# Turning FFN activations and the later x in 32x32 squares on VectorE, with DMAs inside SBUF, instead of on TensorE

## The chip, the cores and the metric

The kernel runs on one core of one Trainium2 chip. The metric is device time in microseconds (us): the median of three runs. One further execution was profiled, and every row shown here is read from that execution. Engines: PE is TensorE (PEld its weight loads), DVE is VectorE, ACT is ScalarE, POOL is GpSimd, SP is SyncE, which here only issues DMAs.

## What is computed

Two layers of an encoder trunk, 256 tokens wide and 2048 channels deep, in float32. Each layer adds to x a mixer, a cross-attention into 256 memory tokens and a SwiGLU FFN with 5632 hidden channels:

```python
for i in range(DEPTH):                       # DEPTH = 2
    h = rms_norm(x, norm_mix_g[i])
    x = x + (retention_na_mixer(h, ...) if i % 2 == 0 else diff_attention_mixer(h, ...))
    m = rms_norm(mem, norm_mem_g[i])
    x = x + memory_cross_attention(rms_norm(x, norm_xattn_g[i]), m, ...)
    x = x + swiglu_ffn(rms_norm(x, norm_ffn_g[i]), w_ffn_in[i], w_ffn_out[i])

def swiglu_ffn(h, w_in, w_out):
    g, u = jnp.split(h @ w_in, 2, axis=-1)
    return (jax.nn.silu(g) * u) @ w_out
```

## The kernel before

Nearly all the time is one long list of matrix products with weights streamed from HBM, walked by `gemm`. Products are made from three matmuls in fp32r on operands split into a high and a low part (`hi*wh + hi*wl + lo*wh`). A **unit** is two 128-row slices of a weight block, for both halves of the 256 tokens: 2 x 2 x 3 = 12 matmuls of 128x512. A 1 MB weight tile `raw` serves two units. For each unit `prepare` has SP load `raw` (every second unit), ACT copy it to `wh` and DVE subtract `wl`. It runs up to three units ahead of the PE. `raw`, `wh` and `wl` have three buffers each. So the copy of one unit waits for the matmuls of the unit three before it, and the load of a `raw` waits for the subtraction of the unit five before the first of its own two.

The stationary operand of a matmul is the activation, channels on partitions, while results and x have tokens on partitions. So activations have to be turned. `turn` does that with four PE transposes (matmuls against an identity) into one PSUM tile `pt` for a half of a 512-column block, and both halves make 8 transposes for a block. Then ACT and DVE split the tile into its two parts: `gained` (with a gain per channel) for x, `split` for FFN activations.

Such work beside the main stream is held in generators run by `side`: `side.pump` after each unit lets one ready step be written, `yield n` puts the rest off by n units, and `side.drain` writes what a later unit needs. The framework's scheduler then moves instructions within each engine's list by its own reckoning, so that the order in the built program is not that of the code. Each engine, SP included, runs its list strictly in order.

The places that the change touches, each with four blocks of 512 channels of x or with one block of activations:

- **memory feed**: after `w_out`, x is turned into `hTx`, used by the product with `w_xq`. The eight units with `w_xkv` (columns 0 to 511) stand between, on the turned memory `mT`. Once in each layer. Here the units of `w_xkv` are called K1 to K8.
- **FFN feed**: during and after `w_xo` (8 units, two for each block) x is turned into `hTf`, used by `w_ffn_in`. Once in each layer. The first units of `w_ffn_in` are F1, F2, F3.
- **next-layer feed**: during the last `w_ffn_out` of layer 0, x is turned into `hT` of layer 1. Once. That product has 24 units: G1 to G24. Block 0 is complete after G10, block 1 after G12, block 2 after G18, block 3 after G24.
- **activations**: 11 blocks in each layer, one for every 16 units of `w_ffn_in`, turned by `act_T` into `aT`, used by `w_ffn_out`.

`x_block(b)` is block b of x in SBUF for both token halves, and `add_x` adds a finished product to it on DVE.

Of the kernel before, what the change touches and what calls it, by code (L numbers as in the profile page):

```python
# [10 lines left out]
F32 = mybir.dt.float32  # L11
# [5 lines left out]
P = 128  # L17
D = 2048
T = 256
# [4 lines left out]
SCALE = HD ** -0.5  # L24
LAM_INIT = 0.8 - 0.6 * math.exp(-0.3 * 1)
NEG = -1e30
FFN_GROUPS = ((0, 4), (4, 8), (8, 11))

OPENING = {2: (2, 3), 4: (-1,), 6: (4, 5), 8: (-2,), 10: (6, 7), 12: (-3,), 14: (-4,)}
# [51 lines left out]
def trunk_kernel(  # L81
# [8 lines left out]
    nc = tc.nc  # L90
# [9 lines left out]
    qk = pool("qk", 1)  # L100
    vp = pool("vp", 2)
# [3 lines left out]
    m8 = pool("m8", 1)  # L105
# [35 lines left out]
    for q in range(2):  # L141
        lo_v, hi_v = wmask[64 * q:64 * q + 64, 0:48], wmask[64 * q:64 * q + 64, 16:64]
        nc.gpsimd.affine_select(lo_v, lo_v, pattern=[[1, 48]], compare_op=ALU.is_ge,
                                fill=NEG, base=8, channel_multiplier=-1)
        nc.gpsimd.affine_select(hi_v, hi_v, pattern=[[-1, 48]], compare_op=ALU.is_ge,
# [8 lines left out]
    def gain(i, layer, k):  # L154
        c = i * 32 + layer * 16 + k
        return gcol[:, c:c + 1]
# [58 lines left out]
    side = Side()  # L215
# [24 lines left out]
    for layer in range(2):  # L240
        j = layer // 2
# [84 lines left out]
    def square_sum(dst, src):  # L326
        junk = sqp.tile([P, NB], F32, tag="sq", name="junk")
        nc.scalar.activation(junk, src, AF.Square, accum_out=dst)

    def turn(srcs, u):  # L330
        pt = ps_t.tile([P, 2, T], F32, tag="pt", name="pt")
        for j in range(2):
            for t in range(2):
                c = (2 * u + j) * P
                nc.tensor.transpose(pt[:, j, t * P:(t + 1) * P], srcs[t][:, c:c + P], ident)  # L335
        return pt

    def gained(dst, kt, src, g):
        hi, lo = dst[0][:, kt], dst[1][:, kt]
        nc.scalar.activation(hi, src, AF.Copy, scale=g)  # L340
        nc.vector.scalar_tensor_tensor(out=lo, in0=src, scalar=g, in1=hi.bitcast(F32),
                                       op0=ALU.mult, op1=ALU.subtract)
# [20 lines left out]
    def finished(tasks):  # L363
        tasks = list(tasks)
        return lambda: all(t["done"] for t in tasks)

    def feed(dst, b, u, srcs, gi, layer, ssr, then=None):
        pt = turn(srcs, u)
        for j in range(2):
            k = 4 * b + 2 * u + j  # L370
            gained(dst, k, pt[:, j], gain(gi, layer, k))
        square_sum(ssr[0][:, u, b:b + 1], srcs[u])
        if then:
            then()
        return
        yield

    def feed_x(dst, b, gi, layer, ssr, wait=0):

        then = (lambda: finish_rstd(ssr)) if b == 3 else None  # L380
        t0 = side.add(feed(dst, b, 0, x_block(b), gi, layer, ssr), wait)
        return [t0, side.add(feed(dst, b, 1, x_block(b), gi, layer, ssr, then), wait + 1, finished([t0]))]

    def split(hi, lo, src):
        nc.scalar.copy(hi, src)
        nc.vector.tensor_sub(lo, src, hi)
# [299 lines left out]
    def finish_rstd(ssr):  # L686
        ss, rstd, r2 = ssr
        nc.vector.tensor_reduce(r2, ss, axis=AX.X, op=ALU.add)
        rsqrt_mean(rstd, r2, D)
        nc.vector.tensor_mul(r2, rstd, rstd)  # L690

    def x_block(b):
        return [x_sb[:, t, b * NB:(b + 1) * NB] for t in range(2)]
# [7 lines left out]
    hT = pair(which[0], "hT")  # L701
    ssr = new_ss("ssx")
    tasks = [side.add(feed_first(hT, u), 2 * u - 2, lambda u=u: u in xts) for u in range(8)]
# [11 lines left out]
    for layer in range(2):  # L715
        j = layer // 2
        A, B = which
        oT = pair(B, "oT")
        if layer % 2 == 0:
            gate = retention_na(j, hT, ssr[1:], oT, gate)  # L720
            kts = (8, 12, 0, 4)
        else:
            nc.vector.scalar_tensor_tensor(out=tabs, in0=tdiff, scalar=-1.0, in1=tdiff, op0=ALU.mult, op1=ALU.max)
            gate = diff_attention(j, hT, ssr[1:], oT, gate)
            kts = KT4

        mT = pair(A, "mT")
        m_v = mem[0].rearrange("(t p) d -> p t d", p=P)

        def mem_block(b):  # L730
            if layer == 0:
                mb = [att.tile([P, NB], F32, tag="att", name="mb") for _ in range(2)]
                for t in range(2):
                    nc.sync.dma_start(mb[t], m_v[:, t, b * NB:(b + 1) * NB])
            mts = [att.tile([P, 2, T], F32, tag="att", name="mt") for _ in range(2)]
            for u in range(2):
                nc.sync.dma_start(mts[u], mem_t[:, 4 * b + 2 * u:4 * b + 2 * u + 2])
            yield 2
            for u in range(2):
                feed_turned(mT, 2 * b + u, mts[u], 2, layer)  # L740
                yield 1
            if layer == 0:
                if b == 3:
                    side.drain(mtasks[:3])
                yield from block_sums(mb, b, mssr)

        mtasks = [side.add(mem_block(b)) for b in range(4)]

        gemm(kts, oT, lambda b, acc: add_x(acc, b), gate=gate)
        side.drain(mtasks)  # L750
        hT = pair(B, "hTx")
        ssr = new_ss("ssx")
        tasks = [t for b in range(4) for t in feed_x(hT, b, 1, layer, ssr, 1 if b == 3 else 0)]

        g = {"wait": 3}

        def epi_k(b, acc):
            g["k"], g["tk"] = normed_T(acc, mssr[1:], c_xk + layer, "kT")

        def epi_q(b, acc):  # L760
            g["q"], g["tq"] = normed_T(acc, ssr[1:], c_xq + layer, "qT")

        def epi_v(b, acc):
            g["v"] = tokens(acc, mssr[1:])

        gemm(KT4, mT, epi_k)
        gemm(KT4, hT, epi_q, gate=by_unit(tasks))
        xo = m8.tile([P, 2, 4, T], F32R, tag="m8", name="xo")
        xo = (xo[:, 0], xo[:, 1])
        heads = [side.add(attend(g, h, xo, h), cond=prepared(g)) for h in range(4)]  # L770
        gemm(KT4, mT, epi_v, steps=2)
        hT = pair(B, "hTf")
        ssr = new_ss("ssx")
        tasks = []

        def epi_xo(b, acc):
            add_x(acc, b)
            tasks.extend(feed_x(hT, b, 3, layer, ssr, 2))

        gemm((0,), xo, epi_xo, gate={0: heads[:2], 1: heads[2:]}, steps=2)  # L780
        gate = by_unit(tasks)

        def act_T(aT, zs, kt):
            for u in range(2):
                pt = turn(zs, u)
                split(aT[0][:, kt + 2 * u:kt + 2 * u + 2], aT[1][:, kt + 2 * u:kt + 2 * u + 2], pt)
                if u == 0:
                    yield 0

        for g0, g1 in FFN_GROUPS:  # L790
            aT = pair(A, "aT")
            n = g1 - g0
            sgs, atasks = {}, []

            def epi_in(i, acc):
                blk = i // 2
                r1 = ssr[1]
                if i % 2 == 0:
                    sgs[blk] = [zp.tile([P, NB], F32, tag="z", name="sg") for _ in range(2)]
                    for t in range(2):  # L800
                        nc.scalar.activation(sgs[blk][t], acc[t], AF.Silu, scale=r1[:, t:t + 1])
                    return
                for t in range(2):
                    nc.vector.scalar_tensor_tensor(out=sgs[blk][t], in0=acc[t], scalar=r1[:, t:t + 1],
                                                   in1=sgs[blk][t], op0=ALU.mult, op1=ALU.mult)
                atasks.append(side.add(act_T(aT, sgs[blk], 4 * blk), 2))

            gemm(KT4, hT, epi_in, gate=gate)
            gate = None
            kts = tuple(4 * b for b in range(n))  # L810
            last = g1 == 11
            side.drain(atasks[:-1])
            if last and layer == 0:
                hN = pair(B, "hT")
                ssn = new_ss("ssx")
                tasks = []

            def epi_out(b, acc):
                add_x(acc, b)
                if last and layer == 0:  # L820
                    tasks.extend(feed_x(hN, b, 0, 1, ssn, 1))
                elif last:
                    for t, xb in enumerate(x_block(b)):
                        nc.scalar.dma_start(out[0][t * P:(t + 1) * P, b * NB:(b + 1) * NB], xb)

            gemm(kts, aT, epi_out, gate={2 * n - 2: atasks[-1:]})
        if layer == 0:
            hT, ssr = hN, ssn
            gate = by_unit(tasks)
        which = which[::-1]  # L830
# [34 lines left out]
```

## Time and profile before

| | |
|---|---|
| median of 3 runs | 2511.26 us (2511.05 to 2512.06) |
| profiled execution | 2511.57 us |
| its span, first to last instruction | 2509.8 us |
| PE busy | 2493.7 us, 99% of the span |
| PEld / DVE / ACT busy | 82% / 57% / 47% |
| HBM read | 465.91 MB, 186 GB/s |
| granted PE clock | 1.00 |

Busy time counts what an engine executes; of the PE it is modelled, since matmuls overlap, and so a busy PE is not proof of a PE at its peak. The rows of groups give line, engine, operation, output and inputs with shapes, count, then busy us, mean ns of one, and idle time before them with what ended it. The rows of the timeline give start us, length us, engine, line, operation and count, and in brackets idle time before. `SPq` is SP issuing a DMA.

### The profile page before, as it was taken

The numbers are of one execution on the slowest core, as the hardware profiler recorded it, in microseconds if no ns is written. First come the engines' busy times: TensorE is split into PE (matmuls) and PEld (weight loads), VectorE is DVE, ScalarE is ACT, GpSimd is POOL, SyncE is SP. The second block draws the span as 40 slices with busy tenths as digits, with TensorE's granted clock in tenths as the row PEclk, the third lists the DMA queues.
The fourth block names the chain that finished last, engine by engine and source line by source line (L and its number), as shares of the span: only waits on it lengthen the run. The fifth ranks groups of instructions, "written<-read, shape, count | busy, mean of one in ns | idle before, by whom it ended". The sixth has DMA issues, their size and how long they took to land.

```text
span 2509.8 us, 28710 instructions
## 1 busy us (share of the span) xinstructions
PE 2493.7 (99%) x11504; PEld 2067.5 (82%) x11504; DVE 1427.0 (57%) x1681; ACT 1187.0 (47%) x1538; POOL 50.6 (2%) x55
## 2 busy tenths in 40 slices
PE   8999999999999999999999999999999999999999
PEld 6888888888888888888888888888888888888887
DVE  6775565674545445544557766757654545455454
ACT  5554464564443444344445555645544444443443
POOL 1000000000000000000000000000000000000000
PEclk9999999999999999999999999999999999999999
DMA  8545566545555555555555555554555655556554
GB/s 285 183 159 182 186 220 200 168 163 190 186 189 195 188 197 185 190 196 185 185 185 167 168 169 179 199 190 155 183 184 188 197 186 196 189 185 200 186 189 163
DMA packets 236742, 469.87 MB, mean 187 GB/s; under 512 B 8128, under 2 KB 8768, under 8 KB 236608
## 3 DMA queue, kind: packets, MB, share of 16 engines
q1 hardware_dynamic: 233808, 463.50, 55.9%
q0 software_dynamic: 640, 2.10, 0.4%
q10 hardware_dynamic: 2160, 2.44, 0.3%
q8 instruction: 90, 1.47, 0.2%
q14 instruction: 44, 0.36, 0.0%
HBM read 465.91 MB, written 2.10 MB: 186 GB/s over the span
## 4 chain that ended last, share of the span: by engine, by line
PE 97%; DMA 1%; DVE 1%; ACT 0%; issue 0%; POOL 0%; ACTq 0%; DVEq 0%; POOLq 0%
PE acc L311 31%; PE acc L313 31%; PE acc L312 31%; PE pt L335 2%; DMA x_sb<-in_x 1%; PE pt L501 0%; PE pa_s L393 0%; PE pa_s L392 0%; PE pa_s L391 0%; PE pa_r L551 0%; DVE wl L286 0%; DMA dec<-in_ret_decay_bwd 0%; DMA lrow<-in_lambda_k 0%; PE pa_o L393 0%; PE pa_o L392 0%
## 5 line engine op out<-in xcount | busy, mean ns | idle before, releaser
L286 DVE TENSOR_TENSOR wl<-raw,wh 128x1024 fp32r<-128x1024 f32 (+1 forms) x865 | 1056.5, 1223 | 954.3 <-ACT wh L285 953.7
L285 ACT CAST wh<-raw 128x1024 fp32r<-128x1024 f32 (+1 forms) x865 | 910.3, 1052 | 1190.7 <-PE acc L313 1162.7
L311 PE MATMUL acc<-wh,hTfh 128*128 128x512 f32 x1408 | 551.5, 392 | 0.0
L313 PE MATMUL acc<-wh,hTfl 128*128 128x512 f32 x1408 | 548.5, 390 | 0.0
L312 PE MATMUL acc<-wl,hTfh 128*128 128x512 f32 x1408 | 547.9, 389 | 0.0
L311 PE MATMUL acc<-wh,hTh 128*128 128x512 f32 x832 | 331.9, 399 | 9.7 <-ACT wh L285 8.2
L312 PE MATMUL acc<-wl,hTh 128*128 128x512 f32 x832 | 325.6, 391 | 1.4 <-DVE wl L286 1.4
L313 PE MATMUL acc<-wh,hTl 128*128 128x512 f32 x832 | 325.6, 391 | 0.0
L313 PEld LDWEIGHTS acc<-wh,hTfl 128*128 128x128 f32 x1408 | 264.2, 188 | 55.6
L312 PEld LDWEIGHTS acc<-wl,hTfh 128*128 128x128 f32 x1408 | 264.4, 188 | 54.0
L311 PEld LDWEIGHTS acc<-wh,hTfh 128*128 128x128 f32 x1408 | 264.4, 188 | 53.8
L311 PE MATMUL acc<-wh,aTh 128*128 128x512 f32 x704 | 275.5, 391 | 0.0
L313 PE MATMUL acc<-wh,aTl 128*128 128x512 f32 x704 | 274.5, 390 | 0.0
L312 PE MATMUL acc<-wl,aTh 128*128 128x512 f32 x704 | 274.1, 389 | 0.0
L311 PEld LDWEIGHTS acc<-wh,hTh 128*128 128x128 f32 x832 | 156.9, 189 | 39.7 <-ACT wh L285 8.2
L313 PEld LDWEIGHTS acc<-wh,hTl 128*128 128x128 f32 x832 | 156.6, 188 | 33.8
L312 PEld LDWEIGHTS acc<-wl,hTh 128*128 128x128 f32 x832 | 157.0, 189 | 32.2 <-DVE wl L286 2.9
L313 PEld LDWEIGHTS acc<-wh,aTl 128*128 128x128 f32 x704 | 132.2, 188 | 27.7
L312 PEld LDWEIGHTS acc<-wl,aTh 128*128 128x128 f32 x704 | 132.2, 188 | 26.8
L311 PEld LDWEIGHTS acc<-wh,aTh 128*128 128x128 f32 x704 | 132.2, 188 | 26.9
L311 PE MATMUL acc<-wh,oTh 128*128 128x512 f32 x256 | 100.2, 391 | 0.0
L313 PE MATMUL acc<-wh,oTl 128*128 128x512 f32 x256 | 99.7, 390 | 0.0
(184 smaller groups left out, 1875.8 us busy)
## 6 DMA issues: line engine op xcount, KB each, us to landing
raw<-in_w_ffn_in SPq DMA_DIRECT2D x176, 1024.0 KB, 5.1
raw<-in_w_ffn_out SPq DMA_DIRECT2D x88, 1024.0 KB, 5.1
raw<-in_w_in_ab SPq DMA_DIRECT2D x55, 1024.0 KB, 5.2
raw<-in_w_in_c SPq DMA_DIRECT2D x48, 1024.0 KB, 5.2
raw<-in_w_out_ab SPq DMA_DIRECT2D x16, 1024.0 KB, 5.2
raw<-in_w_xkv SPq DMA_DIRECT2D x16, 1024.0 KB, 5.0
raw<-in_w_out_c SPq DMA_DIRECT2D x16, 1024.0 KB, 5.1
raw<-in_w_xq SPq DMA_DIRECT2D x8, 1024.0 KB, 5.2
```

What stands on the lines that cost most here:

```text
L285: nc.scalar.copy(wh[:, js], raw[:, rs])
L286: nc.vector.tensor_sub(wl[:, js], raw[:, rs], wh[:, js])
L311: nc.tensor.matmul(acc[t], lhsT=hi[:, kt, ts], rhs=wh[:, j], start=first and j == 0, stop=False)
L312: nc.tensor.matmul(acc[t], lhsT=hi[:, kt, ts], rhs=wl[:, j], start=False, stop=False)
L313: nc.tensor.matmul(acc[t], lhsT=lo[:, kt, ts], rhs=wh[:, j], start=False, stop=last and j == 1)
L335: nc.tensor.transpose(pt[:, j, t * P:(t + 1) * P], srcs[t][:, c:c + P], ident)
```

## The change

`regroup` takes the place of `turn` in two users. It has DVE transpose each 32x32 square within a block for each token half (two instructions a block, into a tile `zt`), and then SP issues 16 DMAs from SBUF to SBUF, each from 32 partitions of `zt` to 32 partitions of `zT`. With tokens_whole (the feeds of x) a DMA writes runs of 32 floats, 128 bytes; without (activations) runs of 1 KB. Both tiles are called `zz` in the profile; they borrow room from tiles that are idle at the time. The splitting steps, as many as before, then read `zT` in SBUF instead of `pt` in PSUM, five units later (MOVE). `turn` stays for q, k and the gated retention output.

```diff
+MOVE = 5
-    def feed(dst, b, u, srcs, gi, layer, ssr, then=None):
-        pt = turn(srcs, u)
-        for j in range(2):
-            k = 4 * b + 2 * u + j
-            gained(dst, k, pt[:, j], gain(gi, layer, k))
-        square_sum(ssr[0][:, u, b:b + 1], srcs[u])
...
+    def regroup(srcs, tokens_whole, room=""):
...
+        for t in range(2):
+            nc.vector.transpose(zt[:, :, :, t], srcs[t].rearrange("p (k j a) -> p j k a", j=4, a=32))
+        for i in range(4):
+            for j in range(4):
+                dst = zT[32 * j:32 * j + 32]
+                nc.sync.dma_start(dst[:, :, :, i] if tokens_whole else dst[:, i], zt[32 * i:32 * i + 32, j])
+        return zT
+
+    def feed(dst, b, srcs, gi, layer, ssr, room):
+        zT = regroup(srcs, True, room)
+        for t in range(2):
+            square_sum(ssr[0][:, t, b:b + 1], srcs[t])
+        if b == 3:
+            finish_rstd(ssr)
+        yield MOVE
+        for k in range(4):
+            gained(dst, 4 * b + k, zT[:, k].rearrange("p t i b -> p (t i b)"), gain(gi, layer, 4 * b + k))
...
-        tasks = [t for b in range(4) for t in feed_x(hT, b, 1, layer, ssr, 1 if b == 3 else 0)]
+        tasks = [t for b in range(4) for t in feed_x(hT, b, 1, layer, ssr, ("", "", "qT", "m8")[b])]
...
-            tasks.extend(feed_x(hT, b, 3, layer, ssr, 2))
+            tasks.extend(feed_x(hT, b, 3, layer, ssr, ("", "", "qT", "kT")[b]))
...
         def act_T(aT, zs, kt):
-            for u in range(2):
-                pt = turn(zs, u)
-                split(aT[0][:, kt + 2 * u:kt + 2 * u + 2], aT[1][:, kt + 2 * u:kt + 2 * u + 2], pt)
-                if u == 0:
-                    yield 0
+            zT = regroup(zs, False)
+            yield MOVE
+            for t in range(2):
+                split(*(x[:, kt:kt + 4, t * P:(t + 1) * P].rearrange("p k (i b) -> p k i b", i=4) for x in aT),
+                      zT[:, :, :, t].rearrange("p i k b -> p k i b"))
...
-                atasks.append(side.add(act_T(aT, sgs[blk], 4 * blk), 2))
+                atasks.append(side.add(act_T(aT, sgs[blk], 4 * blk)))
...
-                    tasks.extend(feed_x(hN, b, 0, 1, ssn, 1))
+                    tasks.extend(feed_x(hN, b, 0, 1, ssn))
```

How it moves instructions is seen in the built lists. First SP's list around both feeds of a layer, before, from the last `w_out` loads to the FFN of layer 0 (`raw<-in_...` are weight loads):

```order
L275 DMA raw<-in_w_out_ab 128x4x512 x12
L275 DMA raw<-in_w_xkv 128x4x512 x4
L275 DMA raw<-in_w_xq 128x4x512 x4
L275 DMA raw<-in_w_xkv 128x4x512 x4
L275 DMA raw<-in_w_xo 128x4x512 x4
L275 DMA raw<-in_w_ffn_in 128x4x512 x32
```

and now, from the last third of the memory feed on:

```order
L276 DMA raw<-in_w_xkv 128x4x512
L389 DMA zz<-zz 32x8x32 x12
L276 DMA raw<-in_w_xkv 128x4x512
L389 DMA zz<-zz 32x8x32 x32
L276 DMA raw<-in_w_xkv 128x4x512
L276 DMA raw<-in_w_xq 128x4x512 x4
L276 DMA raw<-in_w_xkv 128x4x512 x4
L276 DMA raw<-in_w_xo 128x4x512 x4
L276 DMA raw<-in_w_ffn_in 128x4x512
L389 DMA zz<-zz 32x8x32 x64
L276 DMA raw<-in_w_ffn_in 128x4x512 x11
L389 DMA zz<-zz 32x256 x16
```

The third load of `w_xkv` (for K5 and K6) now stands behind 12 DMAs of the feed, the fourth (K7 and K8) behind 32 more, and the second load of `w_ffn_in` (F3 and F4) behind all 64 of the FFN feed. An activation block puts its 16 between two loads.

Next DVE's list at the end of the FFN feed of layer 0 (`x_sb<-acc` adds block 3, `wl` is the subtraction of a unit, `hTfl` the low part made by `gained`), before:

```order
L697 TENSOR_TENSOR x_sb<-acc_4482,x_sb 128x512
L697 TENSOR_TENSOR x_sb<-acc_4483,x_sb 128x512
L286 TENSOR_TENSOR wl<-raw,wh 128x1024
L341 SCALAR_TENSOR_TENSOR hTfl<-pt,gcol,hTfh 128x256 x2
L688 TENSOR_REDUCE ssxq<-ssx 128x2
L320 TENSOR_SCALAR ssxr<-ssxq 128x2
L690 TENSOR_TENSOR ssxq<-ssxr 128x2
L286 TENSOR_TENSOR wl<-raw,wh 128x1024
L341 SCALAR_TENSOR_TENSOR hTfl<-pt,gcol,hTfh 128x256 x2
```

and now:

```order
L719 TENSOR_TENSOR x_sb<-acc_4549,x_sb 128x512
L719 TENSOR_TENSOR x_sb<-acc_4550,x_sb 128x512
L385 STREAM_TRANSPOSE zz<-x_sb 128x16x32 x2
L710 TENSOR_REDUCE ssxq<-ssx 128x2
L321 TENSOR_SCALAR ssxr<-ssxq 128x2
L712 TENSOR_TENSOR ssxq<-ssxr 128x2
L342 SCALAR_TENSOR_TENSOR hTfl<-zz,gcol,hTfh 128x256 x16
L287 TENSOR_TENSOR wl<-raw,wh 128x1024 x16
```

All 16 splitting steps of the four blocks now stand in one run ahead of the subtraction for F3, which is the first `wl` of the last row; ACT's list has its 16 halves in one run at the same place.

Last DVE's list in the next-layer feed, from the add of block 1 on (`hTl` the low part for layer 1), before (the rows after the add of block 1's first half):

```order
L697 TENSOR_TENSOR x_sb<-acc_9026,x_sb 128x512
L286 TENSOR_TENSOR wl<-raw,wh 128x1024
L341 SCALAR_TENSOR_TENSOR hTl<-pt,gcol,hTh 128x256
L286 TENSOR_TENSOR wl<-raw,wh 128x1024
L341 SCALAR_TENSOR_TENSOR hTl<-pt,gcol,hTh 128x256 x2
L286 TENSOR_TENSOR wl<-raw,wh 128x1024
L341 SCALAR_TENSOR_TENSOR hTl<-pt,gcol,hTh 128x256
L286 TENSOR_TENSOR wl<-raw,wh 128x1024 x3
L697 TENSOR_TENSOR x_sb<-acc_9200,x_sb 128x512
L697 TENSOR_TENSOR x_sb<-acc_9201,x_sb 128x512
```

and now:

```order
L385 STREAM_TRANSPOSE zz<-x_sb 128x16x32 x2
L287 TENSOR_TENSOR wl<-raw,wh 128x1024 x4
L342 SCALAR_TENSOR_TENSOR hTl<-zz,gcol,hTh 128x256 x4
L719 TENSOR_TENSOR x_sb<-acc_9404,x_sb 128x512
L385 STREAM_TRANSPOSE zz<-x_sb 128x16x32
L719 TENSOR_TENSOR x_sb<-acc_9405,x_sb 128x512
L385 STREAM_TRANSPOSE zz<-x_sb 128x16x32
L342 SCALAR_TENSOR_TENSOR hTl<-zz,gcol,hTh 128x256 x4
L287 TENSOR_TENSOR wl<-raw,wh 128x1024 x2
L342 SCALAR_TENSOR_TENSOR hTl<-zz,gcol,hTh 128x256 x4
L287 TENSOR_TENSOR wl<-raw,wh 128x1024 x6
```

Between the adds of block 1 and block 2 stood six subtractions, now four; the subtractions for G19 and G20 stand behind the add and the squares of block 2 and the splitting of block 1, and that for G21 behind the splitting of block 2. On SP the tenth `raw` of this product (G19 and G20) stands behind the 32 DMAs of blocks 0 and 1, the eleventh behind the 16 of block 2.

More of the change, by code (lines that the diff above doesn't have):

```diff
@@ L365, in finished, with feed_x @@
         return lambda: all(t["done"] for t in tasks)
-    def feed(dst, b, u, srcs, gi, layer, ssr, then=None):
-        pt = turn(srcs, u)
-        for j in range(2):
-            k = 4 * b + 2 * u + j
-            gained(dst, k, pt[:, j], gain(gi, layer, k))
-        square_sum(ssr[0][:, u, b:b + 1], srcs[u])
[L373 to L382, printed above, removed]
+    def regroup(srcs, tokens_whole, room=""):
+        if room == "m8":
+            both = m8.tile([P, 2, 4 * T], F32, tag="m8", name="zz")
+            zt, zT = both[:, 0], both[:, 1]
+        elif room:
+            zt, zT = (qk.tile([P, 4 * T], F32, tag=room + x, name="zz") for x in "hl")
+        else:
+            zt, zT = (vp.tile([P, 4 * T], F32, tag="v" + x, name="zz") for x in "hl")
+        zt = zt.rearrange("p (j k t b) -> p j k t b", j=4, k=4, t=2)
+        if tokens_whole:
+            zT = zT.rearrange("p (k t i b) -> p k t i b", k=4, t=2, i=4)
+        else:
+            zT = zT.rearrange("p (i k t b) -> p i k t b", i=4, k=4, t=2)
+        for t in range(2):
[14 more added lines that the diff above has]
+            gained(dst, 4 * b + k, zT[:, k].rearrange("p t i b -> p (t i b)"), gain(gi, layer, 4 * b + k))
+    def feed_x(dst, b, gi, layer, ssr, room=""):
+        return [side.add(feed(dst, b, x_block(b), gi, layer, ssr, room))] * 2
     def split(hi, lo, src):
```

## The prediction

> **What bounds the kernel now.** I read the busy times first, then the chain of work that ended last, then the groups, and then the timeline of the places that the change touches.
>
> ```profile
> PE 2493.7 (99%) x11504; PEld 2067.5 (82%) x11504; DVE 1427.0 (57%) x1681; ACT 1187.0 (47%) x1538; POOL 50.6 (2%) x55
> ...
> PE 97%; DMA 1%; DVE 1%; ACT 0%; issue 0%; POOL 0%; ACTq 0%; DVEq 0%; POOLq 0%
> ```
>
> The chain runs through the PE for 97% of the span: matmuls one behind the other. Whatever leaves the PE shortens the kernel by what it takes in that row, and whatever makes the PE wait lengthens it in full. These are the transposes that may go (of the 192 on `sg`, 16 are the gated retention output's and stay):
>
> ```profile
> L335 PE MATMUL pt<-ident,sg 128*128 128x128 f32 x192 | 28.7, 272 | 0.0
> L335 PE MATMUL pt<-ident,x_sb 128*128 128x128 f32 x160 | 24.9, 274 | 0.0
> ```
>
> The PE is fed through a chain that has slack, but not much. In the middle of an FFN product:
>
> ```profile
> 902.16 1.23 DVE L286 TENSOR_TENSOR wl<-raw,wh 128x1024 fp32r<-128x1024 f32 x1 [1.50 <-ACT wh L285]
> 903.30 1.41 DVE L804 SCALAR_TENSOR_TENSOR sg<-acc,ssxr,sg 128x512 f32<-128x512 f32 x2
> ...
> 915.64 1.06 ACT L285 CAST wh<-raw 128x1024 fp32r<-128x1024 f32 x1 [1.66 <-PE acc L313]
> 918.36 1.06 ACT L285 CAST wh<-raw 128x1024 fp32r<-128x1024 f32 x1 [1.66 <-PE acc L313]
> ...
> 903.41 56.71 SPq L275 DMA_DIRECT2D raw<-in_w_ffn_in  x11
> ...
> raw<-in_w_ffn_in SPq DMA_DIRECT2D x176, 1024.0 KB, 5.1
> ```
>
> Copies come 2.72 us apart: that is a unit. A copy waits for the PE and is done 1.06 us later, its subtraction 1.23 us after that, 2.3 us in all, well before the PE comes to it two units on. A `raw` lands 5.1 us after its issue. It is issued when the subtraction five units back is done (one ends at 903.39, at 903.41 SP issues), so 2.3 us after the PE has finished the unit eight back. The copy that needs it starts when the PE has finished the unit three back, five units later: 5 x 2.72 - 2.3 - 5.1 = 6.2 us to spare. With the copy's own 2 x 2.72 - 2.3 = 3.1 us a load may be 9.3 us late before the PE stands.
>
> **What goes.** 22 activation blocks and 5 x 4 blocks of x, 8 transposes each: 336, in 84 groups of four. What a group costs the PE is read from the chain:
>
> ```profile
> 906.48 0.44 PE pt L335 x4
> 909.68 0.44 PE pt L335 x4
> 950.97 0.44 PE pt L335 x4
> ```
>
> From 906.48 to 950.97 are 16 units and two groups: (44.49 - 16 x 2.72)/2 = 0.485 us. 84 x 0.485 = 40.7 us less on the PE. This is the whole gain; nothing leaves ACT or DVE, since the splitting steps are as many as before.
>
> **What comes, and its price.** DVE gets 84 square transposes, and SP 42 x 16 = 672 DMAs. The trace has neither. A transpose of 128x512 lies between the 0.68 us of an add of that shape and the 1.23 us of the 128x1024 subtraction; I take 0.68, as the size is the same, and the sum hardly moves with it, since DVE is idle four tenths of the time. For a DMA three things could set the pace r: SP's issue, the number in flight, and the packets. The rows are from the groups, SP's timeline, the tiles `mb` and `x_sb`, and the DMA queues (from 2.0 to 9.0 us, then over the whole run).
>
> ```profile
> L697 DVE TENSOR_TENSOR x_sb<-acc,x_sb 128x512 f32<-128x512 f32 x80 | 52.0, 683 | 8.1 <-PE acc L313 8.1
> ...
> 7.52 0.38 SPq L275 DMA_DIRECT2D raw<-in_w_in_ab  x1
> 7.94 0.53 SPq L116 DMA_DIRECT2D x_sb<-in_x  x1
> ...
> 13.28 0.98 SPq L125 DMA_DIRECT2D xt<-in_x_t  x2
> 23.14 0.99 SPq L125 DMA_DIRECT2D xt<-in_x_t  x2
> 27.46 3.60 SPq L116 DMA_DIRECT2D x_sb<-in_x  x1
> ...
> L734 SPq DMA_DIRECT2D mb<-in_mem x8: 328/328/341, 239.9 to 339.0; - x8
> ...
> DMA to landing us min/median/max: 2.1/7.3/15.9
> ...
> q10 hardware_dynamic: 432, 0.08, 5.6%
> ...
> q10 hardware_dynamic: 2160, 2.44, 0.3%
> ```
>
> Issue: one alone 0.33 (`mb`) to 0.38 us, two in a row 0.49 each; the size does not matter (the 0.38 is 1 MB, the 0.49 256 KB). In flight: the build has eight DMA semaphores in turn, so a DMA waits for the one eight before it; the fastest landing of the tile x_sb's transfers is 2.1 us, and 2.1/8 = 0.26 us. Packets: a feed's DMA writes 256 runs of 128 bytes, 16 on each of 16 DMA engines. ACT's queue in the first microseconds (from 2.0 to 9.0 us: 432 packets, mean 185 bytes, 5.6% of 16 engines) spent 14.5 ns on a packet: 16 x 14.5 = 0.23 us. Over the whole run its packets (mean 1.1 KB) took 56 ns, which would be 0.9 us. So r lies between 0.26 and 0.9; I take 0.48, SP's issue, because the row of small packets is the nearest and lies below it. The activations' DMAs have two runs of 1 KB on an engine, so SP's 0.48 holds there whatever a small packet costs.
>
> **Activations: hidden.** Where the products end (903.30 to 904.71 us in the rows above) two transposes take until 906.1, 16 issues until 913.8, the last lands about 915.9. The next `raw` in SP's list, due at 903.4 + 5.4 = 908.8, goes out at 914.2: 5.4 us late, of 9.3 spare. The split stands five units later in ACT's and DVE's lists, and ends about 917.8, with the subtraction behind it done at 919.1; the PE wants that one at 903.1 + 7 x 2.72 = 922.1. The cover is 3.0 us. Sum here: 0.
>
> **FFN feed: the PE waits for 64 issues.**
>
> ```profile
> 533.71 0.69 DVE L697 TENSOR_TENSOR x_sb<-acc,x_sb 128x512 f32<-128x512 f32 x1 [0.22 <-PE acc L313]
> 534.62 0.69 DVE L697 TENSOR_TENSOR x_sb<-acc,x_sb 128x512 f32<-128x512 f32 x1 [0.22 <-PE acc L313]
> ...
> 555.52 0.60 PE L335 MATMUL pt<-ident,x_sb 128*128 128x128 f32 x4
> 555.88 0.48 PE L311 MATMUL acc<-wh,hTfh 128*128 128x512 f32 x1
> ```
>
> Block 0 is complete with the first row, the first half of block 1 with the second, and in the new list block 0's second transpose stands behind that: SP can begin at 534.62 + 0.69 + 0.7 = 536.0. The other blocks are complete before SP comes to them. 64 issues end at 536.0 + 64 x 0.48 = 566.7, the second `raw` of `w_ffn_in` at 567.1; it lands at 572.2, copy and subtraction take 2.3: F3 at 574.5. DVE's list says nearly the same: its run of 16 splitting steps stands ahead of that subtraction and waits for the last DMA. Before, F3 began at 555.88, with eight groups ahead of it (the last is shown), so without them at 552.0. The PE stands 22.5 us, in each layer: 45.0.
>
> **Memory feed.**
>
> ```profile
> 428.88 16.69 SPq L275 DMA_DIRECT2D raw<-in_w_xkv  x4
> ...
> 445.09 1.28 DVE L697 TENSOR_TENSOR x_sb<-acc,x_sb 128x512 f32<-128x512 f32 x2
> ...
> 445.38 0.39 PE L311 MATMUL acc<-wh,mTh 128*128 128x512 f32 x1
> ```
>
> K1 starts at 445.38, so K7 at 461.7. The loads of K1 to K8 went out 5.4 us apart from 428.88. Now 12 issues follow the second (434.3 to 440.5), then the third load, then 16 (until 448.7), and block 3, added by 446.4, is turned by about 449.1 behind a subtraction. Its 16 issues end at 456.8, the fourth load goes out by 457.2, and copy and subtraction end at 464.6. The PE stands 2.9 us, twice: 5.8.
>
> **Next-layer feed.**
>
> ```profile
> 1240.98 1.28 DVE L697 TENSOR_TENSOR x_sb<-acc,x_sb 128x512 f32<-128x512 f32 x2
> ...
> 1264.76 1.28 DVE L697 TENSOR_TENSOR x_sb<-acc,x_sb 128x512 f32<-128x512 f32 x2
> ...
> L328 ACT ACTIVATE junk<-x_sb 128x512 f32<-128x512 f32 x48 | 30.2, 629 | 10.3 <-DVE x_sb L697 5.8 <-DVE ss L427 2.1 <-DMA x_sb<-in_x 2.0
> L341 DVE SCALAR_TENSOR_TENSOR hTfl<-pt,gcol,hTfh 128x256 fp32r<-128x256 f32 x32 | 14.3, 477 | 0.0
> ```
>
> Block 2 is added from 1264.76; G19 starts 0.3 us later as K1 does above, and without the four groups between, at 1263.1. Now the subtraction for G19 stands behind that add (1262.8 to 1264.9 with a transpose inside it), ACT's squares of block 2, and the four splitting steps of block 1: 1268.1, then ACT's copy and the subtraction, 1269.9. The PE stands 6.8 us, whatever r is up to 0.58. Then G21: block 2 is turned at 1265.6, 16 issues until 1273.3, load, copy and subtraction until 1281.1; the PE is there at 1269.9 + 5.4 = 1275.3: 5.8 us. Together 12.6. Block 3 comes with 12 units to spare.
>
> **The PE's start after a stand.** At the kernel's beginning matmuls are first twice as far apart:
>
> ```profile
> 10.60 0.63 PE L311 MATMUL acc<-wh,hTh 128*128 128x512 f32 x1
> 11.02 0.63 PE L312 MATMUL acc<-wl,hTh 128*128 128x512 f32 x1
> ...
> 12.66 0.39 PE L313 MATMUL acc<-wh,hTl 128*128 128x512 f32 x1
> 12.88 0.39 PE L311 MATMUL acc<-wh,hTh 128*128 128x512 f32 x1
> ```
>
> 0.42 us apart until 12.6, then 0.23, the slow stretch being 2 to 4 us long: 0.9 to 1.9 us lost. The trace has no stand in its middle, so whether one brings this back is open: 0 to 1.9. I charge 1.5 to the four stands over 5 us, 6.0. The Trainium skill ("TensorE: Matmul & The Clock Gate", Part 1) says that an idle window of about 3.4 us halves the array's clock until some 3.4 us of work have passed; by it each of these stands would cost about 1.7 us, an estimate, 6.8 in all, and the stands of 2.9 us nothing. The slow stretch at the start agrees with it.
>
> **Sum.** -40.7 + 45.0 + 5.8 + 12.6 + 6.0 = +28.7 us. Against the profiled execution's 2511.57 (span 2509.8) that is 2540.3; the median of the runs is 0.3 lower: 2540.0. With r = 0.37 (the shortest issue alone, 0.33, and the 0.04 between the rows of 7.52 and 7.94) the stands are 15.5 twice, 1.1 twice and 10.8: 2520. With r = 0.9 they are 49.4 twice, 20.8 twice and 26.6, with six slow starts: 2646.
>
> **Rivals.** (1) *The small runs are slow*: r above 0.6, from the packets or because full queues hold SP up; at 0.9 the 2646 above. For it: a 128-byte write from SBUF to SBUF is nowhere in the trace, and one x_sb load at the crowded start held SP for 3.60 us; against it the 14.5 ns. 0.13. (2) *Activations wait too*: landing 5.1 us after the issue, as a `raw` does, instead of 2.1 uses up the cover of 3.0; 2 us more in each of 22 blocks give +44, 2584. Against it, the queue is nearly empty there. 0.10. (3) *Faster*: SP issues copies inside SBUF so quickly that the eight in flight set the pace, 0.26. Then the FFN feeds cost 536.0 + 16.6 + 7.8 - 552.0 = 8.4 each, the memory feeds 0, the next layer 9.1, and three slow starts 3.0: 28.9 against 40.7, so 2500. It decides at r below 0.32, where the stands, with four slow starts, sum to 40.7. For it: the packets need only 0.23. Against it: no issue in the trace is under 0.33. 0.16. The Trainium skill ("DMA: Bandwidth & Descriptors", Issuing engines are not separate DMA queues) calls the time that a sequencer takes to initiate a DMA usually small relative to the DMA itself; by that rule it would be this rival. The rows of this trace say the opposite for so small a DMA: 0.48 to issue, 0.23 to move.
>
> **How the numbers follow.** My forecast 0.55, the rivals as said 0.13, 0.10 and 0.16; 0.06 remain for an r about 0.32, no change. A measurement of this kernel tells 0.2%, 5 us, from no change. Slower: 0.78; faster: 0.16; same: 0.06. The forecast's own range is 2520 (r = 0.37) to 2570 (r = 0.6: 30.2 twice, 7.6 twice, 14.5, six slow starts 9.0). For 8 in 10 the range goes from 2497, a little below rival 3, to 2600, beyond rival 2; it leaves out most of rival 1 and a part of rival 3.
>
> **What would show it.** In the new profile: transposes L336 only on `z` and 16 of `sg`; in the chain SP's queue or DMAs of `zz` ahead of F3 with the PE idle some 22 us, at two places 1200 us apart; issues on SP 0.45 to 0.5 us apart; no PE idle in activation blocks; PEclk below 9 at the feeds. It is wrong if issues are closer than 0.35 us, or if the PE's idle time lies in the FFN's 22 blocks.

## The result, and the profile after

The changed kernel takes 2585.36 us (median; 2585.02 to 2588.10), the kernel before 2511.52 us beside it: 1.0296 times the time, 95% interval 1.0278 to 1.0314. That is 73.8 us more, where 28.7 were forecast: the sign and the places where the PE stands are as forecast, the size is not. All times below are such medians; one of the four executions of the kernel with the feeds alone took 8937.17 us, at a granted clock of 1.00, and is left out.

The page of the changed kernel, of its parts the busy times, the clock, the chain and the new DMAs, and from its groups the transposes of `sg` that are left:

```profile
PE 2475.1 (96%) x11168; PEld 2049.0 (79%) x11168; DVE 1473.8 (57%) x1765; ACT 1188.0 (46%) x1538; POOL 51.1 (2%) x55
...
PEclk9999999988999999999989999999799999999999
...
PE 90%; SPq 5%; DMA 3%; DVE 1%; ACT 1%; issue 0%; POOL 0%; ACTq 0%; DVEq 0%; POOLq 0%
...
zz<-zz SPq DMA_DIRECT2D x672, 32.0 KB, 2.0
...
L336 PE MATMUL pt<-ident,sg 128*128 128x128 f32 x16 | 2.4, 272 | 0.0
```

The 336 transposes are gone, but SP's queue and DMAs now hold 8% of the chain, and the clock row dips at the first FFN feed (8 and 8 of ten), the next-layer feed (8) and the second FFN feed (7). PE idle time rose from 2509.8 - 2493.7 = 16.1 to 2583.3 - 2475.1 = 108.2 us, by 92.1. PE busy time fell by only 18.6, not 40.7: some 22 us of the gain went into matmuls at the slow clock.

What the tile `zz` says of the two prices that the trace before could not show (duration in ns, min/median/max), and SP's timeline at both feeds of layer 0:

```profile
L389 SPq DMA_DIRECT2D zz<-zz x672: 512/592/2403, 399.5 to 2525.5; - x168
L385 DVE STREAM_TRANSPOSE zz<-sg x44: 668/687/704, 636.1 to 2515.4; 128x512 f32<-128x512 f32 x44
```

```profile
434.50 8.42 SPq L389 DMA_DIRECT2D zz<-zz  x12
443.02 0.54 SPq L276 DMA_DIRECT2D raw<-in_w_xkv  x1
443.61 21.78 SPq L389 DMA_DIRECT2D zz<-zz  x32
465.49 0.54 SPq L276 DMA_DIRECT2D raw<-in_w_xkv  x1
...
544.72 43.24 SPq L389 DMA_DIRECT2D zz<-zz  x64
588.06 9.27 SPq L276 DMA_DIRECT2D raw<-in_w_ffn_in  x4
```

A square transpose takes 0.69 us (0.68 was taken) and a landing, by the row of the new DMAs above, 2.0 us (2.1 was taken). An issue takes 0.59 us, and 64 of them 43.24: r = 0.676, where 0.48 was taken. The second load of `w_ffn_in` leaves at 588.06. What that does, on ACT and then on the PE:

```profile
589.63 1.71 ACT L341 ACTIVATE hTfh<-zz,gcol 128x256 fp32r<-128x256 f32 x4 [9.06 <-DMA zz<-zz]
...
593.50 1.99 ACT L286 CAST wh<-raw 128x1024 fp32r<-128x1024 f32 x2 [2.16 <-DMA raw<-in_w_ffn_in]
...
594.60 1.22 PE L312 MATMUL acc<-wh,hTfh 128*128 128x512 f32 x2 [27.33 <-ACT wh L286]
```

ACT's last splitting steps of x are done at 591.3. It then waits another 2.16 us for the load that stood behind the 64 DMAs, copies it, and the PE starts F3 after 27.33 us of standing. So x was there first, and the weights ended the wait. Only these last 2.16 us are the load's alone: the first row shows ACT waiting 9.06 us for the feed's own DMAs, and its list has this splitting ahead of the copy. With the load out earlier, by that order, the PE would still have stood some 25 us for the 64 issues; no run tried the load alone.

Where the 73.8 us arise can be read from ACT's weight copies: there are 865 in both kernels, the nth does the same work in both, and it follows the PE by a fixed number of units. First before, then after:

```profile
440.14 1.06 ACT L285 CAST wh<-raw 128x1024 fp32r<-128x1024 f32 x1 [1.66 <-PE acc L313]
...
499.41 1.06 ACT L285 CAST wh<-raw 128x1024 fp32r<-128x1024 f32 x1 [1.66 <-PE acc L313]
...
539.19 1.05 ACT L285 CAST wh<-raw 128x1024 fp32r<-128x1024 f32 x1 [0.33 <-PE acc L313]
...
580.68 1.05 ACT L285 CAST wh<-raw 128x1024 fp32r<-128x1024 f32 x1 [1.67 <-PE acc L313]
```

```profile
439.89 1.05 ACT L286 CAST wh<-raw 128x1024 fp32r<-128x1024 f32 x1 [1.67 <-PE acc L314]
...
508.07 1.06 ACT L286 CAST wh<-raw 128x1024 fp32r<-128x1024 f32 x1 [1.66 <-PE acc L314]
...
547.36 1.06 ACT L286 CAST wh<-raw 128x1024 fp32r<-128x1024 f32 x1
...
621.65 1.05 ACT L286 CAST wh<-raw 128x1024 fp32r<-128x1024 f32 x1 [1.67 <-PE acc L314]
```

The difference after minus before goes from -0.25 to 8.66 over the memory feed of layer 0 (+8.9), then from 8.17 to 40.97 over the FFN feed (+32.8). Taken through the whole list in the same way, saved transposes included (the forecast's column is the stand and its slow start, less 0.485 us for each group):

| place | forecast, us | measured, us |
|---|---|---|
| memory feed, layers 0 and 1 | -1.0 and -1.0 | +8.9 and +8.1 |
| FFN feed, layers 0 and 1 | +20.1 and +20.1 | +32.8 and +32.5 |
| next-layer feed | +11.7 | +13.9 |
| activations, layers 0 and 1 | -10.7 and -10.7 | -10.7 and -10.7 |

The memory feeds, forecast as a small gain, are a loss too. Smaller shifts between the places make up the other -1.3 us to the 73.5 between the two spans.

### The profile page after: what moved, and what is told of

The parts are those of the page before. It is cut to its first block, busy times and chain, and to the rows that moved or that the text cites. A ratio compares the mean times of both kernels' runs of the same rounds, so it can differ in the third digit from the quotient of the medians.

```text
span 2583.3 us, 29105 instructions
## 1 busy us (share of the span) xinstructions
PE 2475.1 (96%) x11168; PEld 2049.0 (79%) x11168; DVE 1473.8 (57%) x1765; ACT 1188.0 (46%) x1538; POOL 51.1 (2%) x55
## 4 chain that ended last, share of the span: by engine, by line
PE 90%; SPq 5%; DMA 3%; DVE 1%; ACT 1%; issue 0%; POOL 0%; ACTq 0%; DVEq 0%; POOLq 0%
PE acc L312 29%; PE acc L313 29%; PE acc L314 29%; SPq L389 5%; DMA raw<-in_w_xkv 1%; PE pt L336 1%; ACT wh L286 0%; DMA raw<-in_w_ffn_out 0%; DMA raw<-in_w_ffn_in 0%; PE pt L523 0%; PE pa_s L415 0%; DVE wl L287 0%; PE pa_s L414 0%; PE pa_s L413 0%; PE pa_r L573 0%
## 5 line engine op out<-in xcount | busy, mean ns | idle before, releaser
L312 PEld LDWEIGHTS acc<-wh,aTh 128*128 128x128 f32 x704 | 133.0, 189 | 40.1 <-ACT wh L286 12.6
```

The costliest lines, as they stand in the source:

```text
L312: nc.tensor.matmul(acc[t], lhsT=hi[:, kt, ts], rhs=wh[:, j], start=first and j == 0, stop=False)
```

## The experiments

The theory: the issues stand in SP's list ahead of weight loads, SP takes 0.65 us for each, and so the loads, and the last blocks of x themselves, come late. The rivals: the 128-byte packets or the bytes hold the queue up; the order of DVE's list does it; the activations carry a part. Below, a "place" is read from matched weight copies as in the table above.

### One part alone

Only `act_T` changed, the feeds as before (e1); and only the feeds changed (e2). The edits put back the old code of the other part:

```diff
-            zT = regroup(srcs, True, room)      # e1: feed as before, by turn
+            pt = turn(srcs, u)
...
-            zT = regroup(zs, False)             # e2: act_T as before, by turn
+                pt = turn(zs, u)
```

> Activations by squares, x by the PE as before. Theory (SP's list: 64 small DMAs at 0.65 us each keep the weight loads back at the feeds of x, and only there): the 44 groups of transposes go for 0.485 us each and nothing takes their place, 2511.5 - 21.3 = 2490. Rival (a part of the loss lies in the 22 activation blocks): with 2 us lost in each, 2534.

> x by squares, activations by the PE as before. Theory: the whole loss is here, and the changed kernel gets its 44 groups back, 2585.4 + 21.3 = 2607. Rival (the activations carry a part): under 2590.

Measured: activations alone 2490.25 us, 0.9916 times the time before (0.9902 to 0.9931); feeds alone 2610.35 us (three executions), 1.0397 (1.0377 to 1.0418). A second measurement of activations alone, on another occasion, gave 2490.19. The PE does not wait in the FFN any more (windows of activations alone; us, busy and matmuls, clock, DMA share, GB/s):

```profile
540.00:600.00 60.00, 60.00 (x276) 1.00 0.55 183
600.00:650.00 50.00, 50.00 (x222) 1.00 0.56 185
```

The gain of 0.485 us a group is real and wholly kept: 21.3 us forecast, 21.0 and 21.2 measured, and 16 issues in a row between two loads are hidden. All of the loss is in the feeds: the rival falls. The feeds alone took 3 us more than expected; the memory feed of layer 1 cost 10.2 us there instead of 8.1.

### Packets and bytes: runs of 1 KB, and half the bytes

e3 lets the feeds' DMAs write the 1 KB layout of the activations; e7 moves two of the four column groups.

```diff
-            zT = regroup(srcs, True, room)      # e3
+            zT = regroup(srcs, False, room)
...
-                nc.sync.dma_start(dst[:, :, :, i], zt[32 * i:32 * i + 32, j])      # e7
+                nc.sync.dma_start(dst[:, 0:2, :, i], zt[32 * i:32 * i + 32, j, 0:2])
```

> The feeds' DMAs write one run of 1 KB to each partition instead of eight of 128 bytes; count and bytes stay. The splitting steps read the tile as it lies, so the tokens of x come out in another order. Theory (an issue on SP takes 0.65 us whatever it moves): 2585, within 6 us. Rival (the 128-byte packets hold the queue up): the issues come closer, 0.5 us apart or less, and at the formulas' 220 us per us of r the kernel takes 2550 or less.

> As many DMAs in the feeds, each with half the bytes and half the runs: only two of the four column groups are moved, and the splitting steps read these twice. Theory (the count decides): 2585, within 6 us. Rival (bytes or packets decide): r falls to about 0.33, 2515 to 2520.

Measured: 2565.65 us (1.0216, 1.0201 to 1.0232) and 2573.06 us (1.0244, 1.0214 to 1.0273). Both miss the 2585 within 6 us that I expected, by 20 and 12 us, and both are well above what the rival gives. SP's timeline of e3 and of e7 at the FFN feed and at the fourth load of `w_xkv`:

```profile
459.35 0.53 SPq L276 DMA_DIRECT2D raw<-in_w_xkv  x1
...
539.73 40.52 SPq L389 DMA_DIRECT2D zz<-zz  x63
```

```profile
459.55 0.53 SPq L276 DMA_DIRECT2D raw<-in_w_xkv  x1
...
539.83 41.74 SPq L390 DMA_DIRECT2D zz<-zz  x63
```

With an eighth of the runs the issues are 40.52/63 = 0.643 us apart, with half the bytes 0.663, against 0.676: the pace hardly depends on what is moved, and the FFN feeds still cost +30.5 and +32.0 (e3), +32.6 and +32.5 (e7). Most of the missing 20 and 12 us lie in the memory feeds (+3.2 and +2.3 in e3, +3.3 and +3.0 in e7, instead of +8.9 and +8.1), and there the list itself came out another way: 4 and 29 DMAs now stand ahead of the third and fourth load of `w_xkv`, where it had been 12 and 32, presumably because the framework's scheduler reckons smaller or plainer DMAs shorter (not shown). The fourth load leaves at 459.4 and 459.6, not at 465.5. In e3 5 us more lie in the next-layer feed (+8.7 instead of +13.9). So the rival falls; but an edit of the data alone had moved instructions too, which the expected numbers leave out. In e3 the splitting of the first columns also waits for fewer DMAs than it did; what of its 20 us that explains was not separated.

### The count: halves and quarters

e5 and e6 move the same bytes in the same runs, in 8 and in 4 DMAs a block.

```diff
+            for I in range(2):                  # e5; e6: zT[:, :, :, i] <- zt[:, i], four times
+                for J in range(2):
+                    for c in range(2):
+                        nc.sync.dma_start(zT[64 * J:64 * J + 64, :, :, 2 * I + c],
+                                          zt[64 * I:64 * I + 64, 2 * J + c])
```

> A feed's block goes in 8 DMAs of 64 partitions instead of 16 of 32: half the issues, the same bytes and the same runs of 128 bytes. The squares come to other partitions than they should. Theory (an issue costs SP 0.65 us whatever its size): r = 0.33 by the formulas, about 2515. Rival (bytes or packets set the pace): 2585.

> A feed's block goes in 4 DMAs of 128 partitions: a quarter of the issues, the same bytes and runs. The squares stay at their partitions. Theory: r = 0.16, FFN feeds 2 us each, memory feeds 0, the next layer still some 7 to 12 us for the order of DVE's list, three or four slow starts of 2: about 2492, faster than before. Rival (bytes or packets): 2585. Rival (the 16 splitting steps ahead of the subtraction in DVE's list cost the time, not SP): over 2550, since they stand there still.

Measured: 2503.86 us (0.9970, 0.9956 to 0.9983) and 2476.22 us (0.9858, 0.9830 to 0.9887). What the tile `zz` says of the feeds' issues (duration in ns, min/median/max), e5 and then e6, and DVE's timeline of e5 at the end of the FFN feed of layer 0:

```profile
L390 SPq DMA_DIRECT2D zz<-zz x160: 590/633/1735, 398.9 to 1775.3; - x160
```

```profile
L388 SPq DMA_DIRECT2D zz<-zz x80: 593/676/4293, 399.7 to 1758.1; - x80
```

```profile
556.37 1.68 DVE L342 SCALAR_TENSOR_TENSOR hTfl<-zz,gcol,hTfh 128x256 fp32r<-128x256 f32 x4 [3.76 <-ACT hTfh L341]
560.58 2.36 DVE L287 TENSOR_TENSOR wl<-raw,wh 128x1024 fp32r<-128x1024 f32 x2 [2.54 <-ACT wh L286]
```

An issue of 64 partitions and 512 runs takes 0.63 us, one of 128 partitions and 1024 runs 0.68, against 0.59 for 32 partitions and 256 runs (medians): the price of one hardly rises. Ten of e6's 80 took over 1 us, up to 4.29; what held these is not shown. The loss goes with the count: FFN feeds of layer 0 +32.8, +13.2, -1.2; next-layer feed +13.9, -2.9, -4.1; memory feeds +8.9, -3.9, -3.9, where -3.9 is a feed with no wait at all. So the bytes were not the cost. Nor was the order of DVE's list at the FFN feed by itself: in e5 the 16 splitting steps still stand in one run ahead of the subtraction for F3 (the rows above are its end), and the place costs 13.2 instead of 32.8. e6 does not speak to that rival, since its list came out with subtractions between the steps. Both kernels are faster than expected, by 11 and 16 us, mainly because the next-layer feed, whose DVE list came out in another order, costs nothing. e6's PE busy time is 2454.7 us, 39.0 less than before: that is the gain term, forecast as 40.7. (In e6 no square changes its partitions, so it is no version to keep.)

### Two queues

e4 sends every second DMA of a feed out on ACT.

```diff
+                queue = nc.scalar if tokens_whole and j % 2 else nc.sync
+                queue.dma_start(dst[:, :, :, i] if tokens_whole else dst[:, i], zt[32 * i:32 * i + 32, j])
```

> Every second DMA of a feed goes out on ACT's queue. Theory (each issuing queue has a pace of its own, 0.65 us): 32 issues on SP, which is r = 0.33 in the formulas of the prediction: FFN feeds 13 us each, memory feeds about 0, next layer 12, five slow starts of 2, less 40.7: about 2520; a few us more where ACT's issues hold back its copies. Rival (what is moved sets the pace: packets, landings, eight in flight): both queues go at half the pace, 2585.

Measured: 2520.32 us (1.0036, 1.0023 to 1.0049). SP's and ACT's timeline at the FFN feed of layer 0:

```profile
532.29 16.06 SPq L390 DMA_DIRECT2D zz<-zz  x24
```

```profile
532.94 10.22 ACTq L390 DMA_DIRECT2D zz<-zz  x15
543.20 0.63 ACT L329 ACTIVATE junk<-x_sb 128x512 f32<-128x512 f32 x1 [10.40 <-DMA zz<-zz]
```

Both queues run side by side at 0.67 and 0.68 us an issue, so what they share does not set the pace; each sequencer has its own. ACT pays for it: its next square of x, and the weight copy behind it, stand for 10.4 us behind 15 issues. The FFN places are +13.7 and +13.4 (measured from the end of the memory feeds), where 13 of stand and 2 of a slow start less 3.9 of saved transposes, 11.1, were expected: the difference is of the size of the few us that the expectation left open for ACT. The total is the expected 2520.

### The price of an issue by itself

e8 has eight series of 16 DMAs behind the kernel's last addition.

```diff
+    for do in (p_square, p_runs, p_all, p_same, p_small, p_hbm, p_hbm_all, p_square2):
+        for i, j in pairs:
+            do(nc.scalar if do is p_square2 else nc.sync, i, j)
```

> The changed kernel with eight series of 16 DMAs put behind its last addition, on two scratch tiles, to read the price of an issue in each form: squares of 32 partitions with one run of 1 KB; with eight runs of 128 bytes; 128 partitions with 256 bytes each; 32 partitions that stay where they are; squares of 32 bytes a partition; 32 partitions from HBM; 128 partitions from HBM; squares again, on ACT's queue. Theory A (any issue in a row costs SP 0.6 us): all series alike. Theory B (a copy from SBUF costs more than a load from HBM): 0.6 for the SBUF series, 0.37 for those from HBM. Theory C (the number of runs or partitions sets it): the series with 128 partitions or eight runs differ from the plain squares by more than 0.1 us. Theory D (what is moved holds the queue up): the squares of 32 bytes go out faster than the rest. Nothing of the kernel's time is read here but the issues behind its end; some 80 us more.

The timeline of SP, from the second series on (eight runs of 128 bytes; 128 partitions; partitions that stay; 32 bytes a partition; 32 partitions from HBM; 128 from HBM), then ACT's; the first series went out among the last loads, so its row is from the tile:

```profile
L864 SPq DMA_DIRECT2D pb<-pa x16: 507/588/673, 2549.4 to 2564.6; - x16
```

```profile
2565.70 10.84 SPq L867 DMA_DIRECT2D pc<-pa  x16
2576.59 10.30 SPq L871 DMA_DIRECT2D pb<-pa  x16
2586.93 10.10 SPq L874 DMA_DIRECT2D pc<-pa  x16
2597.08 10.09 SPq L877 DMA_DIRECT2D pb<-pa  x16
2607.21 9.16 SPq L880 DMA_DIRECT2D pc<-in_x  x16
2616.42 8.37 SPq L884 DMA_DIRECT2D pb<-in_x  x16
...
2609.25 10.50 ACTq L887 DMA_DIRECT2D pc<-pa  x16
```

Per issue that is 0.68, 0.64, 0.63, 0.63, 0.57, 0.52, and 0.66 on ACT. Theory A holds to within 0.1 us: 32 KB or 1 KB, 32 or 128 partitions, 32 or 256 runs, an issue in a long row costs 0.52 to 0.68 us. The cheapest series, 128 partitions from HBM, is the form of the rows from which I took 0.49. D falls outright, C too; of B a tenth of a microsecond is left, not the difference between 0.37 and 0.6.

### Spread out, and only where there is room

e9 keeps squares for the activations and for blocks of x with time to spare, and cuts the issues into groups; e10 is e9 with the next-layer feed back on the PE; e11 is e1 again, on the chip of e10.

```diff
+        zT, moves = regroup(srcs, True, room, True)
+        for i in range(4):
+            moves(i)          # four DMAs
+            yield pause
...
-                    tasks.extend((feed_x(hN, b, 0, 1, ssn, "", 3) if b in (0, 1, 2, 3) else feed_x_pe(hN, b, 0, 1, ssn, 1)))   # e10
+                    tasks.extend(feed_x_pe(hN, b, 0, 1, ssn, 1))
```

> Activations by squares, and of x only the blocks that have room, their issues cut into groups of four with units between: blocks 0 to 2 in the memory feeds, block 3 in the FFN feeds, all four in the next-layer feed; the other blocks go by the PE. In SP's list at most 14, 16 and 20 small DMAs now stand between two weight loads, where it was 32, 64 and 32. Theory (an issue is free as long as the load behind it comes less than 9.3 us late): beside the 44 groups of the activations 24 more groups leave the PE (2 x 3 blocks, 2 x 1, 4; two groups each), 68 x 0.485 = 33.0: 2478.3; up to 4 us more at the run of 20, which takes 13 us. Rival (squares of x cost their wait however they are spread): 2490, the time without them, or more.

> As the kernel before it, with the next-layer feed back on the PE. There the run before had two stands of 6.8 us, ahead of which 20 small DMAs held SP for 14.9 us; matched copies give that place +6.0 us, where activations alone give 0. Theory (bunched issues ahead of a load are the cost, spread ones are free): 2490.4 - 6.0 = 2484.4, some 6 us below activations alone, 16 groups of transposes less. Rival (squares of x are not worth their issues anywhere): 2490.

> Activations alone once more, beside the kernel without the next-layer feed on the same chip: 2490.3 by the first measurement. By the theory the other is 6 us below it, by the rival they are alike.

Measured: e9 2490.43 us (0.9919, 0.9905 to 0.9932), e10 2482.94 us (0.9888, 0.9874 to 0.9901), e11 2490.19 us (0.9915, 0.9902 to 0.9929). From SP's timeline of e9 at the next-layer feed, and of e10 at the FFN feed:

```profile
1230.00 14.88 SPq L389 DMA_DIRECT2D zz<-zz  x20
1244.98 0.54 SPq L276 DMA_DIRECT2D raw<-in_w_ffn_out  x1
```

```profile
550.05 7.78 SPq L389 DMA_DIRECT2D zz<-zz  x12
557.93 1.09 SPq L276 DMA_DIRECT2D raw<-in_w_ffn_in  x2
```

e9 missed its 2478: the 20 in a row took 14.9 us, more stand between the loads after them, and the matched copies show two steps of +6.8 us there (+6.0 for the place in all, where 3.9 saved and at most 4 lost were expected). The expectation of e10 calls these steps stands; the PE itself stood 2.53 and 2.54 us. The total of e9 is thus the rival's 2490, and only the places tell the two apart: at the others (about -2.8 and -1.0 in each layer, the transposes saved) the squares were free, with at most 12 to 14 issues ahead of a load. e10 then came out within 1.5 us of its 2484.4, and 7.3 us below e11 on the same chip. It beats both kernels: 28.5 us less than before.

## Why the prediction was off

**What bounds, and the gain.** Right. 84 groups leave the PE; with hardly a stand in the way (e6) the PE's busy time falls by 39.0 us, and activations alone give 21.0 to 21.2 of the 21.3.

**Activations hidden.** Right, in every run that has them: -10.7 a layer, and in e1 the PE is busy 50.00 of 50.00 us between 600 and 650.

**The price r = 0.48: the step that failed.** The mechanism (SP's issues ahead of the loads) was right, the term was mis-sized. Measured: 0.59 to issue, 0.65 to 0.68 from one to the next. I took two DMAs in a row, from HBM, at the kernel's start, for 64 in a row within SBUF. The timeline of SP before has a longer row, which I passed over:

```profile
1599.28 3.07 SPq L737 DMA_DIRECT2D mt<-in_mem_t  x6
```

It is from HBM too and gives 0.51; in the probe 16 of that form (of 32 KB, not 256) cost 0.52. So the length of the row is some 0.04 of the missing 0.196, and the form of the DMA the rest: roughly, by the probe's series, 0.05 for 32 partitions instead of 128 (0.57), 0.06 for SBUF as the source (0.63), 0.05 for the squares in eight runs (0.68). No row of that form was in the trace, and the forecast's own range of r ended at 0.6.

By the prediction's own steps 0.676 gives: FFN feed, F3 late by 22.5 + 64 x 0.196 = 35.0 us, where 2.96 and 27.33 of stand and 3.2 of slow matmuls between them, 33.5, were found; memory feed, where the 32 issues run on without a gap, fourth load at 465.1 and K7 at 472.5, 10.8 us late, where the trace has 465.49, 472.12 and 10.51; next-layer feed some 17.6 (between its 14.5 at r = 0.6 and 26.6 at 0.9), where 12.3 were found. With its six slow starts of 1.5 that makes 2511.57 - 40.7 + 70.1 + 21.6 + 17.6 + 9.0 = 2589, 4 us from the measured time. That it comes so near is in part luck: these stands sum to 109 us where 92 were found, and the slow starts to 9 where 22 were found.

**The next-layer feed.** 12.6 us in two stands was forecast, 9.11 + 2.66 + 0.52 found; but the first is set by SP (ACT waits its last 2.42 us for the load), since r is past the 0.58 up to which the prediction gives 6.8 to DVE's list. That part of the step could not be tried alone, since the DVE list of e5 and e6 came out in another order.

**The PE's slow start: the second term that was too small.** 1.5 us each for four stands, 6.0, was forecast. There were eight stands over 2 us, and the slow matmuls cost 40.7 - 18.6 = 22 us (20 if the gain is taken as the 39.0 of e6). The timeline of the PE after one of the three under 3 us, at F1 of layer 0, and windows there (the number behind the count of matmuls is the granted clock):

```profile
555.10 0.39 PE L314 MATMUL acc<-wh,xo 128*128 128x512 f32 x1
558.44 0.80 PE L312 MATMUL acc<-wh,hTfh 128*128 128x512 f32 x1 [2.96 <-ACT hTfh L341]
559.03 0.63 PE L313 MATMUL acc<-wl,hTfh 128*128 128x512 f32 x1
...
564.38 0.57 PE L313 MATMUL acc<-wl,hTfh 128*128 128x512 f32 x1
564.78 0.40 PE L314 MATMUL acc<-wh,hTfl 128*128 128x512 f32 x1
```

```profile
555.00:560.00 5.00, 2.04 (x6) 0.79 0.32 51
560.00:565.00 5.00, 5.00 (x13) 0.53 0.33 52
```

14 matmuls take 558.44 to 564.78, 6.34 us instead of 14 x 0.227 = 3.2, so a stand of 2.96 us costs 3.2 more. I had charged nothing for stands that short. Nor does their length alone decide: windows behind a stand of 1.37 us in e4 (it ends at 1250.25), then behind one of 2.53 us in e9 (at 1252.22), each with 0.53 us more two matmuls later:

```profile
1252.00:1256.00 4.00, 3.66 (x10) 0.60 0.61 96
```

```profile
1255.00:1260.00 5.00, 5.00 (x24) 1.00 0.56 184
```

The shorter one was followed by the slow clock, the longer one not; one of 2.54 us later in e9 was (0.63 from 1275 to 1280). What decides is open.

**The sum.** Stands 92.1 instead of 63.4, slow matmuls 22 instead of 6, the gain 40.7 as forecast: 73.4 instead of 28.7. Of the miss 28.7 us lie in the stands, the term that r sets, and 16 in the slow starts.

**The rivals.** (1) small runs: the size of r was its, but not its cause: by e3, e7 and the probe the runs make 0.01 to 0.05 of 0.676. (2) Activations: fell, by e1; that its 2584 is almost the measured time is chance. (3) faster by r = 0.26: no issue of the new form took less than 0.51.

## What to carry to other kernels

Count the instructions that a moved step puts into an in-order queue, and price them from a row of as many of the same form; if the trace has none, take the price at the wide end: here a lone issue (0.33 to 0.38), a pair (0.49) and a row of another form (0.51) were all cheaper than the 0.676 of the new row. A queue that also carries weight loads has room for as many small DMAs between two loads as the lateness that the loads can bear, here 12 to 16 at 0.65 us in 9.3 us and a bit. Spread within that, the blocks that e10 kept were free; all blocks, bunched, cost more than they saved. No run spread all of them, so what spreading does apart from the smaller count is not shown. When an experiment changes only data or shapes, look whether the scheduler has moved the list as well.

## What the runs showed of the hardware

- A DMA in a long row costs its issuing sequencer 0.52 to 0.68 us, from one to the next, whatever it moves up to 32 KB (e8): 0.63 for 1 KB in all, 0.52 from HBM by 128 partitions. One holds SP for 0.59 us with 32 KB in 256 runs, 0.63 with 64 KB in 512 (e5), 0.68 with 128 KB in 1024 (e6), by the medians. The Trainium skill ("Perfetto Trace Analysis", DMA Instruction — HWDGE (DVE, Sync)) says that the sequencer is held until all descriptors of a DMA have been generated; the small rise from 256 to 1024 runs agrees with that, but most of the 0.6 does not follow the runs.
- SP and ACT issue side by side without slowing each other (0.67 and 0.68 in e4).
- A stand of the PE of 2.96 us was followed by a granted clock of 0.53 (560 to 565 us), one of 1.37 us in e4 by 0.60 (1252 to 1256), one of 2.53 us in e9 by 1.00 (1255 to 1260). The rule of some 3.4 us that the prediction drew on ("TensorE: Matmul & The Clock Gate", Part 1, of the Trainium skill) would have left all three without cost; here the measurement decides.
